# Seven quarter products in place of eight in the up projection of the last two token groups, with sums of weight quarters made in the second group

## The chip, the cores and the metric

The kernel runs on one core of a Trainium2 chip. The metric is the device time of one execution in microseconds; of several runs the median is given. The time before is 3064.15 us, the median of three runs from 3063.13 to 3070.54. The engines are named as in the profile: PE is TensorE's matrix multiplication and PEld its loading of weights, DVE is VectorE, ACT is ScalarE, POOL is GpSimd, and SP is SyncE, which issues the DMA transfers here.

## What is computed

One layer of a hybrid decoder, for a prompt of 2048 tokens and for 8 sample sequences with one new token each. A first projection feeds two mixers (a gated linear attention and a dilated sliding-window attention), their outputs are joined and projected back, and a feed-forward part with a squared ReLU follows. The change touches the feed-forward part alone:

```python
mix, c_new, s_new, k_new, v_new = mixer(h, conv_prev, ssm_prev, kb, vb, w_in[l], ..., prompt)
x = x + mix
h = rmsnorm(x, ln_ffn[l])
x = x + jnp.square(jax.nn.relu(h @ w_ffn_up[l])) @ w_ffn_down[l]
```

The model's width is 1024 and `w_ffn_up` is 1024 x 4096, all in 32-bit floats.

## The kernel before, in words

Activations lie transposed, features on the 128 partitions and tokens along the free dimension. The 2056 tokens (prompt and samples) are worked in four groups (`GROUPS`): three of 512, and a last of 520 in two pieces of 260.

**Precision.** A product of 32-bit numbers is made of three products in the faster type `F32R`: each operand is split into a high part (a ScalarE copy that rounds) and a low part (a subtraction), and high x high, high x low and low x high are summed in PSUM. `dense` (L241) does this for one tile of 128 output features: over 8 pieces of 128 inputs, 24 matmuls, each with as many columns as there are tokens (512, or 260 twice).

**Weights.** `load_w` (L223) brings one tile of 128 x 1024 (512 KB) from HBM into `wraw`, lets ScalarE write `whi` (L229) and GpSimd write `wlo` in four quarters (L232). There are three buffers of each, and from the end of group 1 on (function `late`, L1625) a new pool with five `wraw` and three each of `whi` and `wlo`. The new pool lies on the right side of SBUF, where the samples' temporary tiles were. Every few weight loads, a piece of the two caches is copied from HBM to HBM behind the load (`copy_piece`, L1582), until the load 340.

**Stages.** First the input projection of all groups with parts of the mixers (to about 900 us). Then `ffn` (L1563) goes through the four groups. A group has its output projection (`out_proj`, L1451), its norm (`norm2`, L1481, which splits the normed activations into 8 high and 8 low tiles), and eight rounds. A round is four up tiles (`up`, L1524) and one chunk of the down projection (`down`, L1541, four weight tiles, 8 output tiles of 12 matmuls each). The up tiles run four ahead of the down chunk that uses them. The next group's output projection comes before the last down chunk of a group. The norm's scale is applied after the up product: `up` multiplies by `rb` inside the maximum with zero (L1534), squares on ScalarE (L1536), and splits again (L1537, L1538). PSUM has three banks for dense products (`psd`), four for the mixers (`psb`) and one for norms.

**What sets the order.** A planner orders each engine's instructions by priority and by its own costs, and every engine then works through its queue in order. The priorities come in lanes: "feed" (loads, splits, evacuation) ahead of "mixer" ahead of "dense". Mixer work is advanced by one step per ten products (`advance`), so it is interleaved with the products of groups 0 and 1; before group 2's output projection all of it has been issued (`drain`), the decode samples last. Later work such as the next norm and the final norm is advanced by one step per finished product (`next_later`, L85). Tiles of the pool `H` (32 of them, `stile`) hold split activations.

## Time and profile before

| | |
|---|---|
| median of three runs | 3064.15 us |
| the profiled execution's own time | 3051.3 us |
| its span, first to last instruction | 3049.6 us |
| mean granted TensorE clock | 0.981 |
| PE busy | 2922.2 us (96%) |
| DVE, ACT, POOL busy | 1682.6, 1248.5, 1380.4 us |
| moved by DMA | 497.51 MB, mean 163 GB/s |

Group 1 issues its first up load at 1689.7 us and its last down load in front of group 2's output projection at 2135.4 us; group 2's rounds run from about 2214 to 2551 us and group 3's from about 2619 us to the end. A row of the timeline gives start and duration in us, engine, line, operation, the tiles written and read, and the count of merged instructions; in brackets stands the idle time before and what ended it. A row of the groups gives, after the bar, busy time, mean ns of one, and idle time before them. A row of a stretch gives busy time and, in brackets, the number of instructions on each engine, then the granted clock, the mean busy share of the 16 DMA engines and what they moved. A row of the chain gives start, duration and the work that ended last there.

### The profile page before, as it was taken

The page shows a single profiled execution, that of the slowest core. Times are in us where ns is not written, and L with a number is a line of the kernel's source. Part 1 is how long each engine was busy: PE and PEld are TensorE (multiplying, and loading weights), DVE is VectorE, ACT ScalarE, POOL GpSimd, SP SyncE. Part 2 cuts the span into 40 slices and gives each one's busy share as a digit, 9 for nine tenths or more (in the row PEclk, how much of TensorE's full clock was granted, in tenths as well). Part 3 has the DMA queues.
Part 4 walks back from the last instruction along what each step waited for, and adds up shares of the span by engine and source line. Part 5 has one row for each costly group of instructions (what it writes and reads, how often), then busy time and mean ns, then how long its engine had stood idle before and what let it go on. Part 6 is the DMA issues. An engine that isn't in the chain of part 4 may idle for free.

```text
span 3049.6 us, 49363 instructions
## 1 busy us (share of the span) xinstructions
PE 2922.2 (96%) x17793; PEld 2453.3 (80%) x17793; DVE 1682.6 (55%) x4200; ACT 1248.5 (41%) x2624; POOL 1380.4 (45%) x1743
## 2 busy tenths in 40 slices
...
GB/s 154 167 211 219 250 217 162 182 177 143 146 148 196 173 164 147 103 136 140 100 221 252 150 212 214 151 230 248 177 128 190 135 138 162 110 117 92 96 90 77
DMA packets 346643, 497.51 MB, mean 163 GB/s; under 512 B 74776, under 2 KB 245240, under 8 KB 341280
## 3 DMA queue, kind: packets, MB, share of 16 engines
q1 hardware_dynamic: 346400, 494.36, 53.4%
...
## 4 chain that ended last, share of the span: by engine, by line
PE 61%; DVE 4%; DMA 4%; issue 1%; POOL 1%; ACT 1%; SPq 1%; DVEq 0%; POOLq 0%; ACTq 0%
PE dense L251 49%; PE bank L936 2%; PE bank L892 2%; PE bank L949 1%; PE bank L910 1%; POOL wlo L232 1%; DMA dx<-d_dn 1%; PE bank L706 1%; PE bank L708 0%; PE bank L733 0%; PE bank L723 0%; PE bank L742 0%; PE bank L920 0%; DMA dw<-d_gc 0%; DMA dti<-d_t 0%
## 5 line engine op out<-in xcount | busy, mean ns | idle before, releaser
L232 POOL TENSOR_TENSOR wlo<-wraw,whi 128x256 fp32r<-128x256 f32 x1616 | 1269.2, 817 | 1454.0 <-ACT whi L229 868.6
L251 PE MATMUL dense<-s,whi 128*128 128x512 f32 (+2 forms) x8000 | 1689.9, 356 | 27.1 <-ACT whi L229 13.6
L251 PEld LDWEIGHTS dense<-s,whi 128*128 128x128 f32 x8000 | 1301.8, 190 | 237.9 <-issue 19.5
L251 PE MATMUL dense<-s,wlo 128*128 128x512 f32 (+2 forms) x4000 | 887.3, 354 | 0.0
L251 PEld LDWEIGHTS dense<-s,wlo 128*128 128x128 f32 x4000 | 659.6, 190 | 103.8 <-issue 3.7
L229 ACT ACTIVATE whi<-wraw 128x1024 fp32r<-128x1024 f32 x404 | 426.9, 1057 | 699.2 <-PE dense L251 588.3
L1555 DVE TENSOR_TENSOR y<-dense,y 128x512 f32<-128x512 f32 (+1 forms) x320 | 186.4, 583 | 306.1 <-PE dense L251 305.8
L880 ACT ACTIVATE as<-as,as 128x256 f32<-128x256 f32 (+2 forms) x384 | 169.7, 443 | 155.2 <-DVE as L876 153.0
L1534 DVE SCALAR_TENSOR_TENSOR tmp<-dense,rb 128x512 f32<-128x512 f32 (+1 forms) x160 | 93.4, 583 | 231.5 <-PE dense L251 231.0
L876 DVE CUSTOM_DVE_ANT_0 as<-bank,nd 128x256 f32<-128x256 f32 (+2 forms) x384 | 122.1, 350 | 171.3 <-PE bank L936 118.4
L1538 DVE TENSOR_TENSOR s<-tmp,s 128x512 fp32r<-128x512 f32 (+1 forms) x160 | 115.2, 720 | 132.7 <-ACT s L1537 132.6
L1536 ACT ACTIVATE tmp<-tmp 128x512 f32<-128x512 f32 (+1 forms) x160 | 87.6, 548 | 237.0 <-DVE tmp L1534 236.9
L403 DVE SCALAR_TENSOR_TENSOR cy<-cr,cw,cy 128x512 f32<-128x512 f32 (+3 forms) x189 | 148.0, 784 | 29.3 <-ACT cy L401 25.8
L892 PE MATMUL bank<-ident,as 128*128 128x128 f32 (+1 forms) x600 | 110.7, 288 | 3.4 <-ACT as L880 3.1
L892 PEld LDWEIGHTS bank<-ident,as 128*128 128x128 f32 (+1 forms) x600 | 64.1, 137 | 33.2 <-issue 17.4
L936 PE MATMUL bank<-ak,aql 128*128 128x256 f32 x256 | 89.3, 360 | 1.2 <-DVE aql L221 1.1
L1537 ACT ACTIVATE s<-tmp 128x512 fp32r<-128x512 f32 (+1 forms) x160 | 87.4, 547 | 4.5
L936 PE MATMUL bank<-ak,aqh 128*128 128x256 f32 x256 | 88.2, 356 | 0.0
L910 PE MATMUL bank<-ak,aq 128*64 128x64 f32 (+1 forms) x512 | 71.0, 375 | 13.6 <-issue 12.0
L949 PE MATMUL bank<-apt,av 128*64 128x128 f32 x944 | 82.0, 286 | 0.0
L382 ACT ACTIVATE ct<-cy 128x512 f32<-128x512 f32 (+3 forms) x83 | 44.0, 532 | 85.9 <-DVE cy L403 56.1
L383 DVE SCALAR_TENSOR_TENSOR ct<-ct,cy 128x512 f32<-128x512 f32 (+3 forms) x83 | 55.6, 670 | 39.6 <-ACT ct L382 38.8
...
## 6 DMA issues: line engine op xcount, KB each, us to landing
...
wraw<-wup SPq DMA_DIRECT2D x128, 512.0 KB
...
```

The source lines that it names most:

```text
L229: nc.scalar.activation(hi, raw, AF.Copy)
L232: nc.gpsimd.tensor_tensor(out=lo[:, c], in0=raw[:, c], in1=hi[:, c], op=OP.subtract)
L251: self.last = nc.tensor.matmul(p[:, :n], a[:, wo + k * 128:wo + (k + 1) * 128], x[k][:, off:off + n], start=first and i == 0 and k == ks[0 ...
L403: nc.vector.scalar_tensor_tensor(y[:, :np_], r[:, i:i + np_], self.cw[:, j, i:i + 1], y[:, :np_], op0=OP.mult, op1=OP.add)
L876: nc.vector.tensor_tensor_reduce(out=st[:, hh, :nk], in0=b["s"][hh], in1=b["nd"], op0=OP.add, op1=OP.min, scale=-(2.0 ** -(2 * j + hh + 1) ...
L880: nc.scalar.activation(st[:, hh, :nk], st[:, hh, :nk], AF.Exp, bias=so[:, i, hh:hh + 1], scale=-1.0, accum_out=so[:, i, 2 + hh:3 + hh])
L892: nc.tensor.transpose(pT[:m, w * 128:(w + 1) * 128], b["p"][:, hh, kb * 128:kb * 128 + m], self.ident)
L910: nc.tensor.matmul(p[64 * r:64 * r + 64, 256 * hh:256 * hh + nk], qr[hh][:, n:1024:16], ks[hh].bitcast(F32)[:, n:16 * nk:16], start=True, ...
L936: nc.tensor.matmul(p[:, 256 * hh:256 * hh + 256], x[:, q], ks[hh][:, k], start=n == 0, stop=n == 1)
L949: self.nc.tensor.matmul(po[s64, 128 * i:128 * i + 128], v[:, own - (nkb - 1 - kb) * step, s64], b["pt"][:, hh * nkb + kb, :], start=kb == ...
L1538: nc.vector.tensor_tensor(out=ul[:, s], in0=u[:, :n], in1=uh[:, s], op=OP.subtract)
L1555: self.last_v = nc.vector.tensor_tensor(out=y[m][:, s], in0=p[:, :n], in1=y[m][:, s], op=OP.add).ins
```

## The change

Up tiles are taken in pairs, in groups 2 and 3. A pair's 1024 inputs and its two output tiles make four quarters of weights, a11 and a12 (first tile, lower and upper half of the inputs) and a21 and a22 (second tile), each 128 x 512. The activations are four quarters too: lower and upper inputs by first and second half of the tokens (256 or 260). The plain product of a pair is eight products of quarters. The new form takes seven, of sums of quarters (Winograd's form of Strassen's method):

- weight sums: s1 = a21 + a22, s2 = s1 - a11, s3 = a11 - a21, s4 = a12 - s2;
- activation sums, with b11, b12 the lower and b21, b22 the upper inputs: t1 = b12 - b11, t2 = b22 - t1, t3 = b22 - b12, t4 = b21 - t2;
- products a11 b11, s2 t2, a12 b21, s1 t1, s3 t3, s4 b22, a22 t4, each with 4 x 3 = 12 matmuls, and seven additions that put the four quarters of the result together.

In group 1, after each pair of up tiles, `sums_of_weights` makes the four weight sums on GpSimd from the two raw weight tiles, splits s1 and s2 into high and low parts, and stores all to scratch in HBM: s3 and s4 raw (`d_ws`), s1 and s2 as parts (`d_wh`, `d_wl`). Groups 2 and 3 load a11 and a12 as before, the ready parts straight into `whi` and `wlo`, s3 and s4 as raw weights, and a22 as a half tile. The norm in front of these groups makes the activation sums and splits seven sets of four instead of eight tiles. Weight buffers are handed out in turn from lists of pools, with a fourth `wraw` in groups 0 and 1, and seven `wraw`, four `whi` and four `wlo` after, the old three of each among them. Sixteen of the tiles of split activations of groups 2 and 3 lie in a new pool, `H2`. The descriptor scratch in SBUF is reduced to 1024 bytes per partition, which makes room.

```diff
-    def load_w(self, src):
-        nc, W = self.nc, self.W
+    def wtile(self, name, dt):
+        i = self.turns[name] = self.turns.get(name, -1) + 1
+        pools = self.pools[name]
+        pool = pools[i % len(pools)]
+        return pool.tile([128, 1024], dt, name=name, bufs=pools.count(pool))
+
+    def load_parts(self, hi, lo):
         with self.lane("feed"):
-            raw = W.tile([128, 1024], F32, name="wraw", bufs=self.ahead)
-            ins = nc.sync.dma_start(raw, src)
-            hi, lo = [W.tile([128, 1024], F32R, name=n) for n in ("whi", "wlo")]
-            nc.scalar.activation(hi, raw, AF.Copy)
-            for q in range(4):
-                c = slice(256 * q, 256 * q + 256)
+            w = self.wtile("whi", F32R), self.wtile("wlo", F32R)
+            for t, src in zip(w, (hi, lo)):
+                self.nc.sync.dma_start(t.bitcast(F32), src)
+        return w
+
+    def load_w(self, src, step=256):
+        nc = self.nc
+        n = src.shape[1]
+        with self.lane("feed"):
+            raw = self.raw = self.wtile("wraw", F32)
+            ins = nc.sync.dma_start(raw[:, :n], src)
+            hi, lo = self.wtile("whi", F32R), self.wtile("wlo", F32R)
+            nc.scalar.activation(hi[:, :n], raw[:, :n], AF.Copy)
+            for c in range(0, n, step):
+                c = slice(c, c + step)
                 nc.gpsimd.tensor_tensor(out=lo[:, c], in0=raw[:, c], in1=hi[:, c], op=OP.subtract)
...
-        self.later.append(self.norm2(g, y))
+        self.later.append((self.norm2_sums if g > 1 else self.norm2)(g, y))
...
+    def sums_of_weights(self, p, r1, r2):
+        nc, S = self.nc, self.SW
+        a11, a12, a21, a22 = r1[:, 0:512], r1[:, 512:1024], r2[:, 0:512], r2[:, 512:1024]
+        def total(a, b, op):
+            t = S.tile([128, 512], F32, name="wsum", bufs=3)
+            nc.gpsimd.tensor_tensor(out=t, in0=a, in1=b, op=op)
+            return t
+        with self.lane("mixer"):
+            s3 = total(a11, a21, OP.subtract)
+            nc.sync.dma_start(self.d_ws[p, :, 0:512], s3)
+            s1 = total(a21, a22, OP.add)
+            s2 = total(s1, a11, OP.subtract)
+            for i, t in enumerate((s1, s2)):
+                h, l = [S.tile([128, 512], F32R, name=n, bufs=1) for n in ("wsh", "wsl")]
+                self.split(h, l, t, nc.gpsimd)
+                nc.sync.dma_start(self.d_wh[p, :, 512 * i:512 * i + 512], h.bitcast(F32))
+                nc.sync.dma_start(self.d_wl[p, :, 512 * i:512 * i + 512], l.bitcast(F32))
+            s4 = total(a12, s2, OP.subtract)
+            nc.sync.dma_start(self.d_ws[p, :, 512:1024], s4)
+
+    def norm2_sums(self, g, y):
...
+        for k in range(8):
+            while self.have_y <= k:
+                yield 1
+            self.sumsq(y[k][:, :n], n, k, P, "tmp")
+            yield 1
+            if k < 4:
+                continue
+            a, b = tmp(), tmp()
+            for x, i in ((a, k - 4), (b, k)):
+                nc.scalar.activation(x[:, :n], y[i][:, :n], AF.Copy, scale=self.ln2[:, i:i + 1])
+            t, u = tmp(), tmp()
...
+            sub(t1, a[:, m:n], a[:, 0:m])
+            sub(t2, b[:, m:n], t1)
+            sub(t3, b[:, m:n], a[:, m:n])
+            sub(t4, b[:, 0:m], t2)
+            for i, x in enumerate((a[:, 0:m], b[:, 0:m], b[:, m:n], t4, t1, t2, t3)):
+                s = self.H2.tile([128, GW], F32R, name="s2", tag="s2") if count < 16 else self.stile()
+                count += 1
+                h, l = s[:, 0:m], s[:, GW // 2:GW // 2 + m]
+                self.split(h, l, x, nc.vector)
+                sets[i].append((h, l))
+            yield 1
+        yield from self.rms_steps(rb, n, P)
+
+    def up_pair(self, g, p, h2):
...
+        wa = self.load_w(I["wup"][2 * p], 512)
+        ws = self.load_parts(self.d_wh[p], self.d_wl[p])
+        wt = self.load_w(self.d_ws[p], 512)
+        wb = self.load_w(I["wup"][2 * p + 1][:, 512:1024], 512)
+        u = [P.tile([128, GW], F32, name="tmp", tag="tmp") for _ in range(2)]
+        c11, c12, c21, c22 = u[0][:, 0:m], u[0][:, m:n], u[1][:, 0:m], u[1][:, m:n]
+        def product(w, half, i):
+            self.banks += 1
+            bank = self.bank() if self.banks % 7 in (1, 3, 5, 6) else self.psd.tile([128, 512], F32, name="dense", tag="dense")
+            with self.lane("dense"):
+                for j, (a, x) in enumerate(((w[0], 0), (w[0], 1), (w[1], 0))):
+                    for k in range(4):
+                        c = 512 * half + 128 * k
+                        self.last = nc.tensor.matmul(bank[:, :m], a[:, c:c + 128], sets[i][k][x],
+                                                     start=j == 0 and k == 0, stop=j == 2 and k == 3).ins
+            return bank[:, :m]
...
+        def square(x):
+            uh, ul = self.stile(), self.stile()
+            with self.lane("feed"):
+                nc.vector.scalar_tensor_tensor(x[:, :n], x[:, :n], 0.0, rb[:, :n], op0=OP.max, op1=OP.mult)
+                nc.scalar.activation(x[:, :n], x[:, :n], AF.Square)
+                nc.scalar.activation(uh[:, :n], x[:, :n], AF.Copy)
+                nc.vector.tensor_tensor(out=ul[:, :n], in0=x[:, :n], in1=uh[:, :n], op=OP.subtract)
+            out.append((uh, ul))
+        q = product(wa, 0, 0)
+        with self.lane("feed"):
+            nc.scalar.activation(c11, q, AF.Copy)
+        q = product(ws, 1, 5)
+        add(c22, q, c11)
+        add(c11, product(wa, 1, 1), c11)
+        self.next_later()
+        add(c12, product(ws, 0, 4), c22)
+        q = product(wt, 0, 6)
+        add(c21, q, c22)
+        add(c22, q, c12)
+        add(c12, product(wt, 1, 2), c12)
+        square(u[0])
+        add(c21, product(wb, 0, 3), c21)
+        square(u[1])
+        self.next_later()
+        return out
+
+    def ups(self, g, f0, h2, uu):
+        if g > 1:
+            for p in (f0 // 2, f0 // 2 + 1):
+                uu[2 * p], uu[2 * p + 1] = self.up_pair(g, p, h2)
+            return
+        for f in range(f0, f0 + 4):
+            uu[f] = self.up(g, f, h2)
+            if g == 1 and f % 2:
+                self.sums_of_weights(f // 2, self.raw1, self.raw_up)
+            self.raw1 = self.raw_up
...
+        sums = ExitStack()
+        b.SW = sums.enter_context(b.pool("S", 1))
+        b.pools["wraw"] = [W] * 3 + [b.SW]
         def late():
-            b.W, b.ahead = ctx.enter_context(b.pool("W3", 3, side="right")), 5
+            sums.close()
+            W3 = ctx.enter_context(b.pool("W3", 1, side="right"))
+            b.pools = {"wraw": [W] * 3 + [W3] * 4, "whi": [W] * 3 + [W3], "wlo": [W] * 3 + [W3]}
+            b.turns = {}
+            b.H2 = ctx.enter_context(b.pool("H2", 16, side="right"))
             b.out = ctx.enter_context(b.pool("out", 1, side="right"))
...
-    nc = bacc.Bacc("TRN2", target_bir_lowering=False, num_devices=1)
+    nc = bacc.Bacc("TRN2", target_bir_lowering=False, num_devices=1, dynamic_dma_scratch_size=1024)
```

33 lines of the change are left out of this document (28 added, 5 removed).

## The prediction

> **What bounds the kernel now.** I read the head of the page first, then the busy time by stretch of the span, then single instructions in the timeline, the groups by line and shape, the lists of who waited for whom, and the chain of waits.
>
> ```profile
> span 3049.6 us, 49363 instructions
> PE 2922.2 (96%) x17793; PEld 2453.3 (80%) x17793; DVE 1682.6 (55%) x4200; ACT 1248.5 (41%) x2624; POOL 1380.4 (45%) x1743
> q1 hardware_dynamic: 346400, 494.36, 53.4%
> ```
>
> TensorE is the bound over the whole span, and no other engine or the DMA queue comes near it. An average says nothing about one stage, so here are the stretches that the change touches: group 1 from its first up load to its last down load (the first three rows), the change-over to group 2, and four up/down rounds of groups 2 and 3 each.
>
> ```profile
> core 0: us, PE busy (x) PEld busy (x) DVE busy (x) ACT busy (x) POOL busy (x), PEclk, DMA share, GB/s
> 1690.00:1763.00 73.00, 67.71 (x295) 55.02 (x295) 58.84 (x114) 34.07 (x48) 41.54 (x49) 0.95 0.48 153
> 1763.00:2041.00 278.00, 271.72 (x1697) 222.21 (x1696) 164.25 (x450) 85.46 (x162) 120.04 (x156) 0.96 0.64 198
> 2041.00:2136.00 95.00, 85.23 (x363) 68.41 (x362) 69.94 (x105) 25.28 (x30) 50.24 (x57) 0.95 0.73 247
> 2136.00:2192.00 56.00, 46.03 (x215) 37.53 (x214) 33.99 (x51) 14.63 (x20) 23.57 (x28) 0.91 0.49 159
> 2328.10:2506.60 178.50, 178.50 (x770) 144.23 (x769) 44.82 (x64) 54.18 (x64) 97.71 (x128) 1.00 0.42 136
> 2738.00:2922.10 184.10, 184.10 (x1539) 184.10 (x1538) 57.09 (x129) 60.95 (x96) 93.39 (x128) 1.00 0.30 92
> ```
>
> In groups 2 and 3 TensorE never stops, so matmul time removed there is time removed from the span, as long as the others keep up. In the first four rows it is idle for 5.3 + 6.3 + 9.8 + 10.0 = 31.3 us: there other chains sometimes end last, and that is where the change puts its weight sums.
>
> **The products.** Four rounds hold 4 x 192 = 768 matmuls of 512 columns in group 2: 178.5 / 768 = 232.4 ns each; and 4 x 384 = 1536 of 260 columns in group 3: 184.1 / 1536 = 119.9 ns. Group 2's new products have 256 columns. The only matmuls of this line with that width run at the start of the kernel (timeline: start, duration, count):
>
> ```profile
> 20.77 2.06 PE L251 MATMUL dense<-s,whi 128*128 128x256 f32 x16
> 22.67 1.11 PE L251 MATMUL dense<-s,wlo 128*128 128x256 f32 x8
> 23.61 1.23 PE L251 MATMUL bank<-s,whi 128*128 128x256 f32 x9
> ```
>
> From 20.77 to 23.61 are 24 matmuls: 118.3 ns each. A pair of up tiles costs 2 x 24 matmuls in group 2 and 4 x 24 in group 3 today; with seven products of 12 it costs 84 in both. There are 16 pairs. Group 2: 768 x 0.2324 = 178.5 us become 1344 x 0.1183 = 159.0, a gain of 19.5 (by the 260-column row's 119.9 ns it is 17.4). Group 3: 1536 x 0.1199 = 184.2 become 161.1, a gain of 23.1. Together **-42.6 us** (-40.5 to -43).
>
> The weight of a rule here: in the stretch of 260 columns the loads (PEld) are busy all the time too, 1538 of them in 184.1 us. The Trainium skill, page "TensorE: Matmul & The Clock Gate", section "Back-to-back issue gap", says that the spacing in a stream of load and matmul pairs is set by both and gives about 81 ns at 128 columns and 131 ns at 512. An estimate on a straight line between these figures is 98 ns at 256; by it group 2's up projection would grow from 101 to 131 us, the pair of groups would lose 12 us, and halving the columns would not pay. The rows here (232.4, 119.9, 118.3 ns) disagree with it: the spacing follows the columns.
>
> **What feeds the products.** One pair of groups 2 and 3 would take 84 x 0.1183 to 0.1199 = 9.9 to 10.1 us. The rows below are the splits in a down and in an up stretch of group 2 (timeline), and groups by shape of the rounds of groups 3 and 2.
>
> ```profile
> 2442.17 2.83 POOL L232 TENSOR_TENSOR wlo<-wraw,whi 128x256 fp32r<-128x256 f32 x4 [2.69 <-ACT whi L229]
> 2458.64 3.28 POOL L232 TENSOR_TENSOR wlo<-wraw,whi 128x256 fp32r<-128x256 f32 x4 [2.52 <-ACT whi L229]
> 2460.60 0.73 DVE L1538 TENSOR_TENSOR s<-tmp,s 128x512 fp32r<-128x512 f32 x1 [1.36 <-ACT s L1537]
> L1534 DVE SCALAR_TENSOR_TENSOR tmp<-dense,rb 128x260 f32<-128x260 f32 x33 | 14.1, 428 | 39.0 <-PE dense L251 39.0
> L1538 DVE TENSOR_TENSOR s<-tmp,s 128x260 fp32r<-128x260 f32 x32 | 16.3, 509 | 30.1 <-ACT s L1537 30.1
> L1537 ACT ACTIVATE s<-tmp 128x260 fp32r<-128x260 f32 x32 | 13.5, 422 | 1.0
> L229 ACT ACTIVATE whi<-wraw 128x1024 fp32r<-128x1024 f32 x32 | 34.0, 1061 | 82.6 <-PE dense L251 82.6
> L1537 ACT ACTIVATE s<-tmp 128x512 fp32r<-128x512 f32 x16 | 10.1, 632 | 0.5
> ```
>
> GpSimd splits 2560 columns per pair instead of 2048: ten times 256, 7.1 us at 2.83 us per four, 8.2 at 3.28. VectorE: seven additions of a half at 0.43 and, twice, a maximum and a subtraction over 512 at 0.73: 5.9 us. ScalarE: 2.5 casts of 1.06, one copy of 0.42, four passes of 0.63: 5.6 us. All below the pair's 10 us, and the additions hide behind the seven PSUM banks that the products take in turn (a product lasts 1.4 us; if the banks did not hide them, 7 x 0.43 = 3.0 us per pair would show). The 2.83 us splits ran beside a VectorE operation that reads PSUM, the 3.28 us one beside the subtraction with two SBUF inputs. The Trainium skill, page "SBUF — State Buffer", section "Who interferes with whom", says that a VectorE instruction with two SBUF inputs and a GpSimd one that reads SBUF exclude each other for the whole instruction. A pair will hold four of these instead of two; by the rows each costs GpSimd 0.45 us, by the rule up to 0.73, which makes 8.9 or 10.0 us per pair and puts GpSimd level with TensorE. It speaks for the feed rival below.
>
> The sharper limit is the ready-made sums: they go straight into the four whi/wlo buffers. Two weight loads from the chain of waits, and two of SP's waits between 1667 and 2192 us (total, times, longest):
>
> ```profile
> 1622.29 3.78 DMA wraw<-wout
> 2175.43 4.06 DMA wraw<-wout
> SPq L227 <- POOL wlo L232: 181.3, 59, 7.7
> SPq L1392 <- DVE aom L1391: 22.7, 1, 22.7
> ```
>
> A 512 KB load is there 3.8 to 4.1 us after its issue. 92 GB/s take a share of 0.30, so a load holds the DMA engines for 0.524 MB / 307 GB/s = 1.7 us. Of two pairs in a row, the second's sums can be issued when the first's fourth product is done (5.7 us) and are wanted after its first (11.5 us). Two loads: 4.1 and 5.8 us later, high part just ahead of need (5.8), low part with 0.9 us to spare. A load ahead of them in the queue, a cache copy in group 2 among them, makes TensorE wait about 0.8 us, two 2.5 us, for 16 such pairs: 0 to 40 us. All other loads run ahead through seven raw buffers, and over a round of 42.5 us the loads hold the DMA engines for 13 x 1.7 = 22 us. I take **+5 us**, near the lower end, since the DMA share there is 0.30 to 0.42.
>
> The new norm step puts 4 subtractions and 7 splits of a half per pair of tiles on VectorE, about 5.6 us, four times: 22 us per group, against 45 us of output projection and 22 us of the last down product. Exposed is at most the last pair's 5.6 us, twice: 0 to 11, taken as **+2**.
>
> **The sums in group 1.** Per pair six GpSimd operations over 512 columns, two casts, six stores of 256 KB. GpSimd's groups in that stage and elsewhere (busy, mean ns), and one split from the chain of waits:
>
> ```profile
> L232 POOL TENSOR_TENSOR wlo<-wraw,whi 128x256 fp32r<-128x256 f32 x253 | 204.9, 840 | 212.8 <-ACT whi L229 135.5 <-issue 39.6 <-DMA dt<-d_t 7.8
> ...
> L1144 POOL TENSOR_TENSOR ao<-ao,ao 128x512 f32<-128x512 f32 x32 | 42.3, 1322 | 50.3 <-DVE ao L1142 45.0 <-DMA d_v<-vt 4.2
> L1516 POOL TENSOR_TENSOR y<-y,tmp 128x512 f32<-128x512 f32 x2 | 3.4, 1743 | 0.0
> 1609.82 4.40 POOL wlo L232 x4
> ```
>
> By 1.32 to 1.74 us each, 7.9 to 10.4 us per pair, 127 to 167 in all. The first three stretch rows have GpSimd busy for 211.8 of 446 us: it goes to 339 to 379, and still has room. Its queue is in order; behind a sum stands the low part of the next weight, which was begun two tiles ahead of use. That cover is about 10 us (two tiles of 7.4 us in this stage, 446 / 60 loads, less 1.06 and 3.3 to prepare), and one sum is 1.7 us. The 96 stores go through SP, whose weight loads already wait 181 us for buffers there; a store in front of a load that waits for GpSimd delays it by the same 1 to 2 us. The stores move 25 MB, 56 GB/s over the stage: by 0.73 at 247 GB/s the share in the busiest row goes from 0.73 to 0.90. There lies the tail of the decode samples, a chain of transfers and VectorE work which the change-over waits for (chain of waits, and one wait of TensorE):
>
> ```profile
> 2104.84 6.15 DMA d_s<-ass
> 2111.00 3.32 DMA apn<-d_s
> ...
> 2173.70 1.07 PE bank L1384 x8
> ...
> 2179.57 1.07 ACT whi L229
> PE dense L251 <- ACT whi L229: 5.9, 1, 5.9
> ```
>
> Bounds: 0, or all of the 31.3 us of idle time again (and 45 with the rival below). I take **+9**: the tail's transfers of some 20 us stretched by half. On the other side, the last rows show the first output weights of group 2 issued only when the sample tail had ended, and TensorE idle for 5.9 us on them. They went into new buffers on the side of SBUF that the samples held; the changed kernel takes the three old buffers first, which are free. That is **-6** (0 to -6). The smaller scratch area costs nothing: the page's queues are of kinds that the kernel keeps.
>
> **The sum**: -42.6 + 5 + 2 + 9 - 6 = -32.6 us. The profiled execution took 3051.3 us (span 3049.6, 1.7 around it), so it would take 3018.7. The runs' median is 3064.15, 12.9 us above that execution; the same step from it gives **3032 us**, 1.1% less. What a measurement of this kernel can tell from no change is 0.3%, 9 us.
>
> **Rivals.**
> - The sums stretch group 1's chains, and its idle time doubles: +31 instead of +9, and 3054. For it: DMA share 0.73, idle 9.8 of 95 us beside it. Against: GpSimd and DMA have room on average, and the weights are two tiles ahead.
> - The feed of the two-in-a-row pairs is late by two loads each (+40 instead of +5), GpSimd without slack beside it: 3067, no change. Against: a share of 0.30 to 0.42 leaves the queue mostly empty.
> - Slower: both raw weights of a pair stay in their buffers until its last sum, and group 1 has four. Two pairs in a row hold all four, and the next down weight is not loaded before the first pair's chain is done. The second raw lands at 7.4 + 4 us and the down load is due at 4 x 7.4 = 29.6, so 18 us are allowed, 28 with the 10 us of cover; own work and two splits of 3.3 to 4.4 us make 15 to 19. If the chain, queued behind mixer steps and its own stores, takes 37 us, eight rounds lose 9 us each: 72 instead of 9, 3095. From 34 us of chain on (8 x 6 = 48) the kernel is slower than before.
> - Half-width products cost as much per weight load as full ones (group 2's loads are 144.23 / 769 = 187.6 ns): 1344 of them would make 252 us where 178.5 were, in both groups about +74 and +68, and 3200. Group 3's row excludes it nearly, with 119.7 ns per load. The page on TensorE stands behind this one.
>
> **How the numbers follow.** Forecast 0.60 (own range 3018 to 3046), group 1 stretched 0.15, late feed 0.10, slower by held buffers 0.12, load-bound products 0.01, a larger gain than the forecast's range 0.02. Faster by over 0.3% (below 3055): the forecast, the larger gain and half of the second case, 0.69. Within: the other half and most of the third, 0.16. Slower: 0.15. The range has to leave out no more than 0.2: 3014 (all gains, nothing lost, is 3015) to 3067, the late feed.
>
> **What would show it.** The new product line should have 2688 matmuls with 118 to 120 ns from start to start, TensorE without a gap in the up stretches of groups 2 and 3, and rounds of about 42.2 and 43.2 us (178.5 / 4 = 44.6 and 46.0 now). Waits of products for the loads from the sum scratch would show the late feed; waits of the split for raw loads in group 1, and SP waiting for a sum ahead of weight loads, the held buffers; a later end of the sample tail than 2175 us, the stretched group 1. The 5.9 us wait for the first output weight should be gone. The prediction is wrong if the rounds do not shorten, or if group 1 grows by more than 30 us.

## The result and the profile after

The changed kernel takes **3138.28 us** (median of four runs, 3137.04 to 3149.01). The kernel before took 3063.64 us beside it (four runs). The ratio is 1.0251, with a 95% interval of 1.0219 to 1.0282: slower by 2.5%, where 1.1% faster was forecast. The profiled execution took 3137.04 us.

The head of its page:

```profile
span 3135.3 us, 50864 instructions
...
PE 2917.6 (93%) x18177; PEld 2470.3 (79%) x18177; DVE 1889.9 (60%) x4432; ACT 1293.1 (41%) x2712; POOL 1559.4 (50%) x1743
...
q1 hardware_dynamic: 374048, 561.48, 59.0%
```

TensorE is busy for 2917.6 us where it was busy for 2922.2, so the work that the change was to remove is not visible in the total, and 90 us more of the span are idle (217.7 against 127.4). To find them I cut both executions at the same events: the last result of the down projection of each group. The rows of the view by stretch are groups 1, 2 and 3 (span, then busy time of PE, PEld, DVE, ACT, POOL, the granted clock, DMA share, GB/s). Before:

```profile
1723.10:2250.80 527.70, 501.69 (x2710) 408.79 (x2709) 327.67 (x701) 170.91 (x275) 253.87 (x312) 0.96 0.62 198
2250.80:2656.90 406.10, 406.10 (x1949) 337.10 (x1948) 140.18 (x211) 141.69 (x180) 232.81 (x290) 1.00 0.46 148
2656.90:3034.40 377.50, 372.95 (x3093) 371.80 (x3091) 142.05 (x319) 141.37 (x238) 199.08 (x268) 1.00 0.30 95
```

After, with four rounds of group 2 and four of group 3 in the last two rows:

```profile
1739.40:2354.40 615.00, 526.04 (x2707) 422.92 (x2706) 389.63 (x735) 190.90 (x328) 371.50 (x394) 0.91 0.67 209
2354.40:2762.50 408.10, 393.67 (x2530) 357.72 (x2528) 220.87 (x359) 162.89 (x240) 248.81 (x242) 0.98 0.61 197
2762.50:3120.40 357.90, 350.92 (x2901) 349.38 (x2899) 199.30 (x367) 142.59 (x207) 229.24 (x224) 1.00 0.49 154
2473.70:2642.20 168.50, 168.50 (x1059) 151.61 (x1058) 80.82 (x120) 60.16 (x80) 107.33 (x104) 1.00 0.69 218
2833.90:3006.60 172.70, 172.70 (x1442) 172.70 (x1441) 84.66 (x152) 60.36 (x81) 107.44 (x104) 1.00 0.50 159
```

Group 1 takes 87.3 us more, group 2 takes 2.0 more, group 3 takes 19.6 less. Another 16.3 us lie ahead of 1739.4 us. Part of those is only the spread between executions: the profiled execution of before was 12 us below its median, the one of after 1 us.

Two losses add up in the row of group 1. TensorE is idle for 615.0 - 526.0 = 89.0 us instead of 26.0, and the same 2,700 matmuls take 24.3 us longer, with a granted clock of 0.91 instead of 0.96. GpSimd is busy for 371.5 us instead of 253.9.

**What is waited for in group 1 now** (the lists of waits of the changed kernel from 1739.4 to 2354.4 us: us in total, times, longest):

```profile
PE dense L271 <- DVE y L1705: 24.4, 6, 7.9
PE bank L1404 <- DVE savc L1398: 18.3, 4, 12.0
PE bank L683 <- issue: 10.8, 2, 6.2
PE bank L1225 <- issue: 10.6, 1, 10.6
...
SPq L247 <- POOL wlo L252: 188.5, 61, 7.7
...
SPq L247 <- POOL wsum L1525: 29.2, 7, 6.3
SPq L1530 <- POOL wsum L1525: 21.5, 6, 4.7
SPq L1537 <- POOL wsl L226: 19.6, 15, 5.4
...
POOL wlo L252 <- ACT whi L249: 89.0, 23, 18.4
POOL wsum L1525 <- DMA wraw<-wup: 20.7, 6, 4.2
POOL wsl L226 <- DMA d_wl<-wsl: 20.1, 6, 7.6
...
POOL wsum L1525 <- DMA d_ws<-wsum: 17.8, 4, 7.6
```

Nothing here waits much for a sum directly. TensorE waits for VectorE's down results, for the decode samples (L1404, L1225) and for the gated attention (L683). What stands behind the sums is two queues: SyncE holds weight loads back for a sum that still reads a raw tile (29.2 us) and waits for sums to store (41.1 us), and GpSimd, whose queue is in order, stands still inside the sums for a raw weight to land, for ScalarE and for its own stores (L1525 and L226). GpSimd waited for 170.9 us for ScalarE's high parts before and for 89.0 now: it had been early, and is so no longer.

The chain that ends last runs through it (start, duration, work):

```profile
2085.01 1.27 POOL wsum L1525
2086.30 3.39 DMA d_ws<-wsum
...
2098.36 5.04 DMA ss<-sssm
...
2165.27 4.14 DMA d_wh<-wsh
2170.09 5.54 DMA d_wh<-wsh
...
2206.80 9.72 DMA d_s<-ass
```

The decode samples' transfer of `ass` ends at 2216.5 us in place of 2111.0, and it lasts 9.72 us in place of 6.15.

**The sums themselves** cost what was estimated (GpSimd's groups in that stretch: busy us, mean ns, idle time before):

```profile
L226 POOL TENSOR_TENSOR wsl<-wsum,wsh 128x512 fp32r<-128x512 f32 x28 | 38.6, 1380 | 35.3 <-DMA d_wl<-wsl 20.1 <-ACT wsh L225 13.1 <-PE dense L271 1.9
...
L1525 POOL TENSOR_TENSOR wsum<-wraw 128x512 f32<-128x512 f32 x28 | 36.3, 1310 | 52.2 <-DMA wraw<-wup 20.7 <-DMA d_ws<-wsum 17.8 <-issue 13.3
```

1.31 to 1.38 us each, at the lower end of the forecast's 1.32 to 1.74, some 8.1 us a pair and 130 in all.

### The profile page after: what moved, and what is told of

The parts are those of the page before. It is cut to its first block, busy times and chain, and to the rows that moved or that the text cites. A ratio compares the mean times of both kernels' runs of the same rounds, so it can differ in the third digit from the quotient of the medians.

```text
span 3135.3 us, 50864 instructions
## 1 busy us (share of the span) xinstructions
PE 2917.6 (93%) x18177; PEld 2470.3 (79%) x18177; DVE 1889.9 (60%) x4432; ACT 1293.1 (41%) x2712; POOL 1559.4 (50%) x1743
## 5 line engine op out<-in xcount | busy, mean ns | idle before, releaser
L252 POOL TENSOR_TENSOR wlo<-wraw,whi 128x256 fp32r<-128x256 f32 (+1 forms) x1520 | 1319.8, 901 | 1258.7 <-ACT whi L249 680.3
L271 PE MATMUL dense<-s,whi 128*128 128x512 f32 (+2 forms) x6464 | 1445.0, 366 | 46.9 <-DVE y L1705 30.8
L271 PEld LDWEIGHTS dense<-s,whi 128*128 128x128 f32 x6464 | 1086.1, 192 | 240.8 <-DVE y L1705 32.0
L271 PE MATMUL dense<-s,wlo 128*128 128x512 f32 (+2 forms) x3232 | 756.2, 364 | 1.3 <-POOL wlo L252 1.3
L249 ACT ACTIVATE whi<-wraw 128x1024 fp32r<-128x1024 f32 (+1 forms) x436 | 446.7, 1026 | 687.5 <-PE dense L271 418.5
L271 PEld LDWEIGHTS dense<-s,wlo 128*128 128x128 f32 x3232 | 548.7, 191 | 95.7 <-POOL wlo L252 3.7
L896 DVE CUSTOM_DVE_ANT_0 as<-bank,nd 128x256 f32<-128x256 f32 (+2 forms) x384 | 122.0, 350 | 170.8 <-PE bank L956 118.3
L423 DVE SCALAR_TENSOR_TENSOR cy<-cr,cw,cy 128x512 f32<-128x512 f32 (+3 forms) x189 | 147.8, 783 | 29.9 <-ACT cy L421 27.3
L1598 PE MATMUL bank<-s,whi 128*128 128x256 f32 (+1 forms) x1024 | 144.8, 284 | 0.0
L1598 PEld LDWEIGHTS bank<-s,whi 128*128 128x128 f32 x1024 | 133.2, 191 | 0.6
L1598 PE MATMUL dense<-s,whi 128*128 128x256 f32 (+1 forms) x768 | 109.4, 286 | 5.6 <-DMA whi<-d_wh 5.6
L1598 PEld LDWEIGHTS dense<-s,whi 128*128 128x128 f32 x768 | 99.9, 191 | 5.9 <-issue 5.9
L1688 DVE TENSOR_TENSOR s<-tmp,s 128x512 fp32r<-128x512 f32 x64 | 57.9, 905 | 45.0 <-ACT s L1687 45.0
L930 PE MATMUL bank<-ak,aq 128*64 128x64 f32 (+1 forms) x512 | 70.9, 375 | 13.3 <-DMA aq<-d_q 11.6
```

The lines of the kernel that those rows point to most:

```text
L249: nc.scalar.activation(hi[:, :n], raw[:, :n], AF.Copy)
L252: nc.gpsimd.tensor_tensor(out=lo[:, c], in0=raw[:, c], in1=hi[:, c], op=OP.subtract)
L271: self.last = nc.tensor.matmul(p[:, :n], a[:, wo + k * 128:wo + (k + 1) * 128], x[k][:, off:off + n], start=first and i == 0 and k == ks[0 ...
L423: nc.vector.scalar_tensor_tensor(y[:, :np_], r[:, i:i + np_], self.cw[:, j, i:i + 1], y[:, :np_], op0=OP.mult, op1=OP.add)
L896: nc.vector.tensor_tensor_reduce(out=st[:, hh, :nk], in0=b["s"][hh], in1=b["nd"], op0=OP.add, op1=OP.min, scale=-(2.0 ** -(2 * j + hh + 1) ...
L930: nc.tensor.matmul(p[64 * r:64 * r + 64, 256 * hh:256 * hh + nk], qr[hh][:, n:1024:16], ks[hh].bitcast(F32)[:, n:16 * nk:16], start=True, ...
```

## The experiments

Times of a round below go from the last down result of a chunk to the next one's. `first` is group 0's first down result; group 1, 2 and 3 are the stretches as above. All are from the profiled execution. Medians and ratios are from all runs; each ratio is to runs of the kernel before that were taken beside them, whose median lay between 3061.67 and 3069.82 us. In e2, e5, e7, e8, e12, e13, e17 and e18 groups 2 and 3 read the first pair's sums for all pairs, as in e1, so their outputs are not the reference's.

| kernel | median us | ratio to before (95%) | first | group 0 | group 1 | group 2 | group 3 |
|---|---|---|---|---|---|---|---|
| before | 3063.64 | 1 | 1113.2 | 609.9 | 527.7 | 406.1 | 377.5 |
| after | 3138.28 | 1.0251 (1.0219-1.0282) | 1122.7 | 616.7 | 615.1 | 408.0 | 358.0 |
| e1 no sums | 3051.45 | 0.9969 (0.9955-0.9983) | 1124.8 | 617.8 | 528.5 | 404.3 | 358.6 |
| e2 additions only | 3127.18 | 1.0214 (1.0194-1.0234) | 1126.8 | 623.5 | 598.9 | 406.4 | 359.0 |
| e5 no stores | 3141.41 | 1.0253 (1.0231-1.0275) | 1124.5 | 616.8 | 619.2 | 407.3 | 358.0 |
| e6 sums in group 0 | 3106.14 | 1.0146 (1.0128-1.0163) | 1150.3 | 649.5 | 523.9 | 408.3 | 357.9 |
| e7 pinned additions | 3096.22 | 1.0093 (1.0072-1.0114) | 1128.8 | 615.1 | 566.7 | 406.9 | 357.9 |
| e8 pinned fills | 3087.90 | 1.0075 (1.0049-1.0101) | 1121.3 | 617.4 | 562.5 | 407.2 | 359.2 |
| e9 sums on VectorE | 3093.02 | 1.0087 (1.0063-1.0110) | 1121.9 | 620.8 | 566.9 | 407.1 | 357.9 |
| e12 additions that read raw tiles | 3126.17 | 1.0182 (1.0150-1.0213) | 1121.3 | 614.2 | 590.8 | 407.3 | 358.0 |
| e13 chain of sums, constant | 3110.56 | 1.0139 (1.0123-1.0155) | 1126.0 | 616.0 | 587.2 | 407.3 | 358.5 |
| e15 real sums, pinned | 3137.24 | 1.0230 (1.0208-1.0252) | 1132.2 | 618.1 | 613.8 | 404.3 | 357.9 |
| e14 before, small scratch | 3068.18 | 1.0005 (0.9993-1.0016) | 1116.1 | 611.6 | 532.4 | 406.1 | 377.5 |
| e17 seven in group 2 only | 3064.55 | 1.0006 (0.9993-1.0019) | 1119.0 | 613.8 | 531.9 | 404.2 | 376.1 |
| e18 no sums, three raw | 3043.92 | 0.9948 (0.9932-0.9964) | 1121.1 | 620.3 | 519.5 | 406.6 | 358.9 |
| e10 sums in group 2, VectorE | 3073.94 | 1.0022 (1.0007-1.0037) | 1127.5 | 610.8 | 540.7 | 419.8 | 357.5 |
| e16 same, three raw | 3057.18 | 0.9991 (0.9976-1.0005) | 1114.2 | 610.0 | 532.9 | 424.6 | 357.4 |
| e11 sums in group 2, GpSimd | 3124.81 | 1.0210 (1.0192-1.0228) | 1125.1 | 610.6 | 551.3 | 465.9 | 357.0 |
| e19 as e16, sums later | 3060.42 | 0.9998 (0.9983-1.0012) | 1127.0 | 609.6 | 524.2 | 432.8 | 358.4 |
| e20 as e19, more tiles | 3061.50 | 0.9986 (0.9971-1.0001) | 1125.3 | 608.1 | 522.5 | 427.1 | 358.4 |

### Is it the sums at all?

e1 makes the sums of the first pair alone.

```diff
-            if g == 1 and f % 2:
+            if g == 1 and f == 1:
-        ws = self.load_parts(self.d_wh[p], self.d_wl[p])
+        ws = self.load_parts(self.d_wh[0], self.d_wl[0])
```

(and `d_ws` likewise)

> The weight sums of the first pair alone are made in group 1, and all sixteen pairs of groups 2 and 3 read them, so the output is not the reference's; every load and product of groups 2 and 3 stays. Three theories of where group 1's 87 us went: PORT (GpSimd's sums make VectorE operations with two SBUF inputs wait for the shared port, and the chains through VectorE get late), HELD (both raw weights stay in their buffers until the last sum, so weight loads are late), STORES (96 stores in SP's queue and 25 MB more DMA traffic). All three: group 1 returns to about 528 us between the last down results of groups 0 and 1 (615 in the changed kernel), and the total to 3040 to 3060.

3051.45 us, 0.3% faster than before. The sums cost 1.0251 - 0.9969 = 0.0282 of 3064 us, 86 us, and nearly all of it is in group 1. But without them the seven products bring 10 us only, not the 41.6 forecast for everything but the sums (-42.6 + 5 + 2 - 6). Groups 2 and 3 together are 20.7 us shorter in e1 than before; what is missing of these lies ahead of group 2 or in the spread of executions.

### Which part of the sums?

e5 stores the first pair's sums alone (each of the six stores as the one below).

```diff
-            nc.sync.dma_start(self.d_ws[p, :, 0:512], s3)
+            if p == 0:
+                nc.sync.dma_start(self.d_ws[p, :, 0:512], s3)
```

e2 leaves the weights alone and adds a constant tile to itself six times a pair on GpSimd, in place of the sums of pairs 2 to 16.

```diff
+        if p == 0:
+            self.wx = S.tile([128, 512], F32, name="wx", bufs=1)
+            nc.vector.memset(self.wx, 1.0)
+        else:
+            with self.lane("mixer"):
+                for _ in range(6):
+                    total(self.wx, self.wx, OP.add)
+            return
```

> All sums and splits as in the changed kernel, reading and holding the raw weights, but only the first pair's are stored, and all pairs read those; output not the reference's. PORT: 3105 to 3138. HELD: 3110 to 3138, since the raw buffers are held until the last sum (the chain no longer waits for its stores, so perhaps 10 us less). STORES: as without sums, 3040 to 3065.

> As the kernel without sums, but each further pair issues six additions of 512 columns on GpSimd that read one constant tile twice: no raw weight is read or held, nothing is stored. Output not the reference's. PORT: most of the 87 us is there again, total 3100 to 3135. HELD and STORES: as without sums, within 15 us of it.

Without the stores nothing is gained: 1.0253 against 1.0251, group 1 at 619.2 us. So the 25 MB of stores are not the price, even though stores stand in the chain above; when they are gone, other work ends last. e2 could not be read as meant: its additions wait for nothing, so the planner put nearly all of them at the start of group 1 (its first round took 160.2 us in place of the changed kernel's 112.0).

So in e7 the same additions are held to their place, behind the low parts of the pair's second weight in GpSimd's queue (`lo_ins` is the subtraction of L252); e8 has fills there that read nothing from SBUF, of about the same time.

```diff
-            with self.lane("mixer"):
+            with self.lane("mixer"), self.tc.issue_after(self.lo_ins):
```

```diff
-                    total(self.wx, self.wx, OP.add)
+                    t = S.tile([128, 512], F32, name="wsum", bufs=3)
+                    for c in (512, 512, 256):
+                        nc.gpsimd.memset(t[:, 0:c], 1.0)
```

> Six additions of one constant tile to itself per pair again, but queued behind the low parts of the pair's second weight, so that they spread over group 1 as the changed kernel's sums do; nothing read of the raw weights, nothing stored, all pairs read the first pair's sums (output not the reference's). PORT, or GpSimd's queue being longer (QUEUE: low parts of weights and the mixers' own GpSimd steps come late behind the sums): group 1 takes 590 to 615 us, total 3110 to 3140. If the waits for raw weights or for stores inside the sums were what spreads the delay: below 560 us.

> The same places in GpSimd's queue, with fills of 512, 512 and 256 columns in place of each addition: about the same time on GpSimd (1.3 to 1.4 us per group of three), but no SBUF input. PORT: VectorE's operations with two SBUF inputs no longer wait for them, so group 1 is within 25 us of the 528 without sums, total 3050 to 3080. QUEUE: as the pinned additions, 590 us and over, total 3110 to 3140.

Group 1 of e1, of e7 and of e8, by stretch:

```profile
1742.60:2271.20 528.60, 503.19 (x2708) 408.79 (x2708) 343.27 (x736) 177.23 (x300) 256.41 (x308) 0.96 0.63 201
```

```profile
1743.90:2310.70 566.80, 511.28 (x2709) 412.95 (x2708) 389.46 (x736) 176.96 (x300) 351.01 (x398) 0.94 0.59 188
```

```profile
1738.80:2301.30 562.50, 509.38 (x2708) 411.88 (x2707) 353.66 (x736) 177.38 (x300) 359.00 (x578) 0.94 0.60 189
```

95 us more of GpSimd time (351.0 - 256.4) make group 1 38 us longer; 103 us of fills make it 34 longer. So **time in GpSimd's queue alone costs about 0.33 to 0.40 us per us**, with nothing held, nothing stored and nothing waited for, though GpSimd is idle for over 200 us of this stretch. Neither number had been named: the theories gave 590 us and more, or under 560 (e7) and 553 (e8).

The pair also separates the queue from a conflict in SBUF. VectorE executes the same 736 instructions in 343, 389 and 354 us: additions with two SBUF inputs on GpSimd lengthen VectorE's work by 46 us, fills of the same time by 10. The Trainium skill, page "SBUF — State Buffer", section "Who interferes with whom", says that a VectorE instruction with two SBUF inputs contends with a GpSimd one that reads SBUF and not with one that only writes it. The trace agrees in direction; but the two ratios, 1.0093 and 1.0075, lie within each other's intervals. By these intervals the conflict can be some 16 of the 86 us at most (an estimate), so it is not the main cost.

e9 gives the sums, whole, to VectorE.

```diff
-            nc.gpsimd.tensor_tensor(out=t, in0=a, in1=b, op=op)
+            nc.vector.tensor_tensor(out=t, in0=a, in1=b, op=op)
-                self.split(h, l, t, nc.gpsimd)
+                self.split(h, l, t, nc.vector)
```

> The complete computation with the four sums and two splits of a pair on VectorE in group 1 instead of GpSimd: about 0.69 us each where nothing holds the port, 66 us of VectorE in all. PORT: GpSimd's share of the port falls back to that of the weights, but VectorE is itself busy for two thirds of group 1 and its chains get 4 us longer per pair: group 1 560 to 590 us, total 3080 to 3110. QUEUE (GpSimd's length was the cost): 535 to 560 us, 3055 to 3080.

Group 1 falls from 615.1 to 566.9 us, inside the range that PORT had named (560 to 590), though e7 and e8 leave PORT little. Half of the loss goes with GpSimd's queue. The other half stays, with raw tiles held, steps in chain and stores as before, and with the sums now in VectorE's queue; e9 doesn't part these.

### Held raw tiles, the steps in chain, or the place?

e12 and e13 add one thing each to e7. In e12 the additions read the raw weights:

```diff
-                for _ in range(6):
-                    total(self.wx, self.wx, OP.add)
+                for x, y in ((a11, a21), (a21, a22), (a11, a22), (a11, a21), (a21, a22), (a12, a21)):
+                    total(x, y, OP.add)
```

In e13 sums of the constant are made with the dependences of the real ones, two copies on ScalarE and two subtractions behind them:

```diff
+                x = self.wx
+                total(x, x, OP.subtract)
+                s1 = total(x, x, OP.add)
+                s2 = total(s1, x, OP.subtract)
+                for t in (s1, s2):
+                    h, l = [S.tile([128, 512], F32R, name=n, bufs=1) for n in ("wsh", "wsl")]
+                    self.split(h, l, t, nc.gpsimd)
+                total(x, s2, OP.subtract)
```

e15 is the changed kernel whole, with its sums at e7's place:

```diff
-        with self.lane("mixer"):
+        with self.lane("mixer"), self.tc.issue_after(self.lo_ins):
             s3 = total(a11, a21, OP.subtract)
```

> As the kernel with pinned additions of a constant (group 1 took 566.7 us, the kernel 3096), but each of a pair's six GpSimd additions reads two quarters of the pair's raw up weights, so both raw tiles are held until the sixth addition is done. No high and low parts, no stores; all pairs of groups 2 and 3 read the first pair's sums, so the output is not the reference's. HELD (the remaining 50 us of group 1 come from weight loads that wait for a raw tile the sums still read): group 1 at 600 to 620 us, the kernel at 3125 to 3145, and SyncE's queue waits at L247 for GpSimd's sum tile. CHAIN (they come from the steps inside the sums, GpSimd to ScalarE and back): group 1 stays at 560 to 575, the kernel at 3090 to 3102. PLACE (they come from where the planner puts the sums, the pinned kernels being better placed): 560 to 575 as well.

> As the kernel with pinned additions of a constant, but with the dependences of the real sums: the same four sums, two copies to high parts on ScalarE and two subtractions on GpSimd that wait for them. The operands are a constant tile, so no raw weight tile is held; no stores; groups 2 and 3 read the first pair's sums, so the output is not the reference's. CHAIN: group 1 at 600 to 620 us, the kernel at 3125 to 3145. HELD or PLACE: group 1 at 565 to 580 (ScalarE's 30 copies are new, at most 15 us of it), the kernel at 3090 to 3108.

> The changed kernel whole, with its sums put behind the low parts of the pair's second weight in GpSimd's queue, as the pinned additions were. PLACE: group 1 at 565 to 580 us, the kernel at 3092 to 3108. HELD: as the changed kernel, group 1 at 605 to 620, the kernel at 3128 to 3145. CHAIN: the same as HELD here; the two kernels beside it tell those two apart.

In ratios to before, times 3064: from e1 to e7 38.0 us, from e7 to e12 27.3, from e7 to e13 14.1. Together 79 us, a ratio of 1.0228, and e15 measured 1.0230. Place is therefore no part of it that the intervals show (e15 and the changed kernel overlap), and held tiles and steps in chain both are; each theory had claimed the whole. (The profiled execution of e12 is the shortest of its four, 3108.17 us, so its group 1 of 590.8 us shows less than the median, 3126.17, does.)

The wait that e12 was to show (SyncE's queue, 1690 to 2320 us, us in total, times, longest):

```profile
SPq L247 <- POOL wlo L252: 123.4, 40, 7.3
SPq L247 <- POOL wsum L1525: 116.7, 14, 17.8
```

In e7 no row like the second is among the ten largest waits of SyncE's queue, and the first is 258.7 us. So the queue doesn't wait longer in e12 (240.1 us for both rows): the row shows which work frees a raw tile last, and the cost is read from the times alone. A caution on the sizes: e12's additions also keep GpSimd busy for 31 us more than e7's, and e13's steps for 24 us more (382.5 and 374.6 us against 351.0). At e7's 0.40 us per us that would be 13 of the 27 us, and 9 of the 14. So the 86 us are divided as: GpSimd's time 33 to 60, held raw tiles 14 to 27, steps in chain 5 to 14, and some 7 between e15 and the changed kernel that the intervals don't resolve.

e6 makes the sums, whole, in group 0.

```diff
-            if g == 1 and f % 2:
+            if g == 0 and f % 2:
```

> The complete computation, with the weight sums made in group 0's up projection instead of group 1's. There VectorE is busy for about 35 and GpSimd for about 25 of 76 us, TensorE for 76. PORT: the sums find both engines with room, 3040 to 3070. HELD: TensorE has no idle time in group 0 and a round lasts longer (86 us for 8 loads), so little, 3045 to 3075. STORES: little, DMA share 0.35 to 0.5 there. A loss like group 1's (3110 and over) would speak for a cost of the sums that does not depend on what runs beside them.

They cost 0.0177 of 3064, 54 us, there: 25 us ahead of the first down result, where group 0's first up tiles lie, and 32 behind it. Cheaper than in group 1, and still far more than groups 2 and 3 give. The 3106 us lie above the ranges of all three theories (up to 3075) and near the 3110 that were to speak for a cost that does not depend on what runs beside the sums.

### The parts that were costed at nothing

e14 is the kernel before with the change's smaller descriptor scratch, e18 is e1 without the fourth raw tile of groups 0 and 1.

```diff
-    nc = bacc.Bacc("TRN2", target_bir_lowering=False, num_devices=1)
+    nc = bacc.Bacc("TRN2", target_bir_lowering=False, num_devices=1, dynamic_dma_scratch_size=1024)
```

```diff
-        b.pools["wraw"] = [W] * 3 + [b.SW]
```

> The kernel before with the one other line of the change: the scratch for DMA descriptors cut to 1024 bytes. The changed kernel and all its variants reach group 0's first down result at 1122.7 to 1127.5 us (1150.3 where group 0 makes the sums) against 1113.2 before. SCRATCH (the small scratch costs it): 3072 to 3077 us and the first down result at 1120 to 1128. PLAN (it comes with the other order and the fourth raw tile): 3061 to 3066 and 1112 to 1115.

> The kernel whose sums are those of the first pair alone, without the fourth raw weight tile in groups 0 and 1 (3051 us, first down result at 1124.8 us, group 1 at 528.5). The output is not the reference's. FOURTH (the fourth tile costs the early time): 3038 to 3045 and a first down result at 1113 to 1119. PLAN (nothing but the order of an execution and of the plan): 3048 to 3055, and 1119 to 1127.

The scratch costs nothing (1.0005). Its trace also is another execution of what is in effect the kernel before, and it has group 1 at 532.4 us, so that of the 87 us some 5 are spread. The fourth raw tile is no help but a loss: 0.9948 without it against 0.9969 with it, 6 us, and from e10 to e16 below 0.0031, 9.5 us. In both pairs group 1 becomes shorter, by 9.0 and 7.8 us; the first down result moves by 3.7 and 13.3, so that theory's number for it was met in one of the two. The intervals of e1 and e18 still overlap, so the 6 us stand less firmly than the 9.5. Why a tile more makes it longer was not tried further.

### Where group 2's gain went

e17, without the sums of further pairs like e1, takes seven products in group 2 and eight in group 3, so that in group 2's last rounds the old norm runs.

```diff
-        self.later.append((self.norm2_sums if g > 1 else self.norm2)(g, y))
+        self.later.append((self.norm2_sums if g == 2 else self.norm2)(g, y))
-        if g > 1:
+        if g == 2:
```

> The kernel whose sums are those of the first pair alone (3051 us; group 2 took 404.3 us, its rounds 67.0, 49.6, four at 42.1, 48.1, 71.2), with seven products in group 2 only: group 3 computes eight as in the kernel before, so its operands are made by the old norm. The sums of pairs 2 to 16 are not made, so the output is not the reference's. NORM (VectorE's work on the operands of group 3, made in group 2's last rounds, delays the down results): round 6 falls from 48.1 to 42 to 44 and group 2 to 395 to 400. FEED (it is loads): round 6 stays at 47 to 49. Round 1 at 49 to 50 in either (its matmul waits for a high part). Group 3 at 376 to 379; the kernel at 3060 to 3070.

The rounds of group 2 were 68.3, 44.8, 44.6, 44.4, 44.6, 44.7, 44.6, 70.1 us before; 69.4, 49.9, 42.2, 42.1, 42.2, 42.0, 49.0, 71.2 after; and in e17 66.9, 49.9, 42.2, 42.1, 42.2, 42.0, 48.4, 70.5. Round 6 stays, so NORM falls: it is not the new norm. TensorE's waits in group 2 of e17 name two places:

```profile
PE dense L1598 <- DMA whi<-d_wh: 6.1, 2, 5.8
PE dense L271 <- DVE y L1705: 4.7, 1, 4.7
```

Round 1 is the first: the ready part of s2 for the second pair. In the changed kernel (timeline of TensorE):

```profile
2433.64 1.11 PE L1598 MATMUL bank<-s,whi 128*128 128x256 f32 x8
2434.59 0.63 PE L1598 MATMUL bank<-s,wlo 128*128 128x256 f32 x4
2440.42 2.05 PE L1598 MATMUL dense<-s,whi 128*128 128x256 f32 x8 [5.19 <-DMA whi<-d_wh]
2442.26 1.05 PE L1598 MATMUL dense<-s,wlo 128*128 128x256 f32 x4
2443.12 1.91 PE L1598 MATMUL bank<-s,whi 128*128 128x256 f32 x8
2444.82 0.99 PE L1598 MATMUL bank<-s,wlo 128*128 128x256 f32 x4
2445.65 1.11 PE L1598 MATMUL dense<-s,whi 128*128 128x256 f32 x8
```

Eight matmuls take 1.11 us before the stall and 2.05 after it; the granted clock is 0.50 from 2440.4 to 2445.6 us, and 1.00 ahead of the stall and behind that stretch. So the stall of 5.2 us costs 7.7 in all (49.9 - 42.2). The Trainium skill, page "TensorE: Matmul & The Clock Gate", section "Part 1: The HAM clock gate (the "warmup" mystery)", says that after one idle window of about 3.4 us the clock is halved until a window of work has passed. The trace agrees: the stall is longer than that, and the half clock lasted 5.2 us.

What made the part late stands in SyncE's queue. Its load was issued at 2429.1 us, behind six cache copies of 512 KB issued from 2418.8 to 2424.8, and the 16 DMA engines were busy all the time until TensorE went on (a share of 1.0 from 2418.8 to 2440.3 us). In e1, e5, e7, e15 and e17 the same six copies stand ahead of the same load, and TensorE waits 5.8 to 6.3 us there. In the later rounds at most three copies stand so close ahead of a part, and no such wait comes. A kernel without the bunch was not run.

Round 6 is the second wait: the down results wait in VectorE's queue behind low parts of `m`, the inputs of group 3's output projection, which come late. The loads of `m` before (all eight within 8.3 us, and ScalarE waits 3.2 us for them) and in the changed kernel (18.0 us, 9.7):

```profile
L1435 SPq DMA_DIRECT2D m<-d_mix x8: 319/350/557, 2563.4 to 2571.7; - x8
...
  ACT s L220: 3.2, 4
```

```profile
L1455 SPq DMA_DIRECT2D m<-d_mix x8: 376/382/424, 2656.9 to 2674.9; - x8
...
  ACT s L225: 9.7, 4
```

In e17 three of them are issued by 2565.6 us and the other five from 2579.8 on, behind four output weights in SyncE's queue, which wait for GpSimd to free their raw tiles. Before, one output weight stood between them. That the late `m` are the cause is read from this order and was not tried by itself. Nor do seven raw tiles explain the order alone: e20 below has seven in group 2 as well, with plain products, and there one output weight stands between the loads of `m`, as before. What in the new form puts four there stays open.

### Can the sums be made elsewhere and win?

In group 2 TensorE was the only bound, and six raw tiles are in turn there; so e10 makes the sums in group 2, on VectorE, and takes seven products in group 3 alone. e16 is e10 with three raw tiles in groups 0 and 1; e11 is e10 with the sums on GpSimd.

```diff
-            if g == 1 and f % 2:
+            if g == 2 and f % 2:
-        if g > 1:
+        if g > 2:
```

(the pool of the sums is kept to the end of group 2, and the tiles of the seven operands follow it)

> The complete computation with the sums on VectorE in group 2, whose up projection stays plain, and seven products in group 3 alone. No mixer runs in group 2 and VectorE is busy for a quarter of it (44.8 of 178.5 us), so the 66 us of sums fit under TensorE's work. Expected by PORT and QUEUE both: group 1 as without sums (528), group 2 405 to 412, group 3 358 (19 less than before): 3035 to 3055, faster than the kernel before by 5 to 25 us. If the stores' 25 MB or held raw buffers cost: group 2 over 420.

> Whole and exact: seven products in group 3 alone, sums on VectorE in group 2 (3074 us with four raw tiles in groups 0 and 1), now with three raw tiles there as in the kernel before. FOURTH: 3060 to 3066, so no slower than before, group 1 at 527 to 533. PLAN: 3070 to 3077.

> Whole and exact: seven products in group 3 alone, sums on GpSimd in group 2, where six raw tiles are in turn. With VectorE's sums group 2 took 419.8 us and the kernel 3074. QUEUE and HELD both say that GpSimd's 10 additions and subtractions of about 1.1 us for a pair (22 us in a round of 45) and the raw tiles held by them delay the low parts of the weights, but group 2 has free time on GpSimd: group 2 at 425 to 450, the kernel at 3080 to 3105. If GpSimd is idle enough there: 406 to 415, the kernel at 3058 to 3068.

e10 missed its expectation: group 2 took 419.8 us and not 405 to 412. On GpSimd the sums cost even more there than was expected: group 2 at 465.9 us, 60 above before. The stretch in e11 and in e16:

```profile
2287.10:2753.00 465.90, 421.43 (x1949) 345.41 (x1948) 151.19 (x246) 159.46 (x231) 324.76 (x364) 0.96 0.51 170
```

```profile
2257.00:2681.60 424.60, 411.66 (x1942) 339.38 (x1941) 202.88 (x320) 161.45 (x230) 230.67 (x282) 0.98 0.57 185
```

Against the kernel before, GpSimd is busy for 92 us more in e11 (324.8 against 232.8) and the stretch is 60 us longer, 0.65 us per us. The whole sums in group 1, after against e1, made 86 us (615.0 - 528.6) of 115 (371.5 - 256.4), 0.75. So they are hardly cheaper in a stage where TensorE alone was the bound. On VectorE group 2 takes 419.8 and 424.6 us, 14 and 18 more than before, against 20 less in group 3. Of e16's 18.5 us, 12.9 are idle time of TensorE and 5.6 are its matmuls at a granted clock of 0.98 in place of 1.00. e16, at 0.9991, and e20 below, at 0.9986, are the best versions that compute the whole, and neither is faster beyond its interval. In group 2 of e16, 2257 to 2640 us, VectorE's queue stands still for raw weights, with an up result behind:

```profile
DVE y L1705 <- PE dense L271: 70.3, 35, 3.5
DVE wsum L1525 <- DMA wraw<-wup: 61.0, 11, 7.1
```

e19 puts a pair's sums behind the low part of its second up result (`low` is the subtraction of L1688); e20 gives them more tiles as well, in a pool that is opened at the end of group 1.

```diff
-        with self.lane("mixer"):
+        with self.lane("mixer"), self.tc.issue_after(self.low):
             s3 = total(a11, a21, OP.subtract)
```

```diff
-            t = S.tile([128, 512], F32, name="wsum", bufs=3)
+            t = S.tile([128, 512], F32, name="wsum", bufs=4)
-                h, l = [S.tile([128, 512], F32R, name=n, bufs=1) for n in ("wsh", "wsl")]
+                h, l = [S.tile([128, 512], F32R, name=n, bufs=3) for n in ("wsh", "wsl")]
-            b.pools = {"wraw": [W] * 3 + [b.SW] + [W3] * 2, "whi": [W] * 3 + [W3], "wlo": [W] * 3 + [W3]}
+            b.pools = {"wraw": [W] * 3 + [b.SW] * 2 + [W3] * 2, "whi": [W] * 3 + [W3], "wlo": [W] * 3 + [W3]}
```

> Whole and exact: seven products in group 3 alone, sums on VectorE in group 2, three raw tiles in groups 0 and 1 (3057 us, group 2 at 424.6 us with rounds of 46 to 48), with the sums of a pair now put behind the low part of the pair's second up result in VectorE's queue, so that no up result stands behind a sum that waits for a raw weight. ORDER (that wait is the cost): rounds at 44.4 to 45.2, group 2 at 406 to 414, the kernel at 3038 to 3048, faster than the kernel before. HELD (the raw tiles held longer cost as much): 46 to 48 a round, the kernel at 3054 to 3062. TIME (six operations of 0.69 us a pair): the same as HELD.

> Whole and exact: the kernel with the sums of group 2 put behind the up results (3060 us, group 2 at 432.8 us), with three tiles for each part of a sum in place of one, four for the sums in place of three, and one raw tile more, in memory that is free in group 2. STORES (VectorE's waits for the parts' stores are the cost): group 2 at 406 to 416, the kernel at 3040 to 3050, faster than the kernel before by 0.4 to 0.7%. TIME (six operations of 0.69 us a pair and their place between the results): group 2 stays at 420 to 433, the kernel at 3053 to 3063.

The waits for raw weights are gone in e19, and 78.1 us of waits for the parts' stores have come in their place (2270 to 2690 us); in e20 those are gone too, and group 2 is still at 427.1.

```profile
DVE wsl L226 <- DMA d_wl<-wsl: 78.1, 20, 6.0
```

Two rounds of e19 came down to 44.6 and 45.4 us, and its rounds 0 and 1 went up to 78.1 and 52.6 (72.9 and 49.5 in e16). So ORDER and STORES fall as the whole cause: waits that went were replaced by others. In e20 VectorE still does six more operations a pair among results that TensorE needs emptied from its three dense banks; whether their time or their place sets the rest stays open.

## Why the prediction was wrong

**The products' time** was right. Group 2's four rounds hold 384 matmuls of 512 columns and 672 of the products: (168.5 - 384 x 0.2324) / 672 = 117.9 ns each, forecast 118.3. Group 3's: (172.7 - 768 x 0.1199) / 672 = 120.0. Rounds of 42.1 and 43.2 us, forecast 42.2 and 43.2. The rival by which halved columns would not pay is out, and with it the estimate from the page "TensorE: Matmul & The Clock Gate", section "Back-to-back issue gap", of the Trainium skill.

**Group 3's gain** was nearly right: 19.6 us of 23.1. Its round 0 gained 0.7 where two rounds' worth of up tiles should have given 5.8; TensorE waits 3.8 us for the norm's scale there (1.5 before). In group 2's round 0 the waits for it went from 0 to 3.4, and it lost 1.1 where 4.9 were to be gained. That is the norm step: +2 in the sum for both groups, and 5 to 6 in each, of which the waits show 2 to 3.

**Group 2's gain** was given back: -19.5 + 5 + 2 came out as +2.0. Four rounds gave their 9.8. The feed term (+5) had the right mechanism: a pair's second part came late behind cache copies, which the forecast had named. But it was one wait of 5.2 us behind six copies, and not many small ones in 16 pairs, and the slow matmuls behind the stall made it 7.7; that the sizes are near is partly luck. GpSimd was not level with TensorE: its splits took 7.0 us a pair (five of 1.40), not the 8.9 or 10.0 that the forecast weighed. The step that failed is "All other loads run ahead through seven raw buffers": the loads of `m` did not, by the order in the queue they stood behind output weights, and round 6 took 6.8 us more than the rounds before it (49.0 - 42.2). The forecast had no term for them.

**The sums in group 1** are the main error: +9 came out as +86 (after against e1). The operations and their durations were right. The step that failed is "GpSimd busy for 211.8 of 446 us: it goes to 339 to 379, and still has room", with a cover of "about 10 us" against "one sum is 1.7 us". The room is an average, and the cover was counted for one sum, not for the six of a pair in the same queue; 130 us of work went into a queue whose low parts and mixer steps are on the way to TensorE. Each us of it cost 0.33 to 0.40 by its time alone, and 0.75 with all that the sums hold and wait for. Through which steps the delay reaches TensorE is not shown one by one: TensorE itself waits only 1.3 us for a low part in the changed kernel's group 1. I priced only the transfers of the samples' tail, and e5 shows that transfers were not it.

**The slower rival** named a real mechanism, held raw tiles, and the sign: +72 and 3095 by it. Measured alone it is 14 to 27 us; the rest came from what it and the other rivals took as given. It had reckoned with a chain of 37 us for a pair; in the changed kernel a pair took 13 to 41 us from its first sum to its last, and once 80. The rival that doubled group 1's idle time (+31) had the right kind: idle time went from 26 to 89 us, more than threefold.

**The early output weights** (-6): the wait of 5.9 us is gone from the list, and the last round went from 81.0 to 70.7. But in e1 round 6 went from 52.9 to 61.9; rounds 6 and 7 together are 133.9 before and 132.7, so 1 us and not 6; against e14, another execution of the old order, with 57.5 + 80.8 = 138.3, it would be 5.6. So the gain lies between 1 and 6 us and is not settled.

**At nothing**: the scratch was right (e14), the fourth raw tile was not (6 to 9.5 us, e18 and e16); it had no term in the sum at all.

What the forecast named as proof of its being wrong is what happened: group 1 grew by more than 30 us.
